# Two transformer blocks in one kernel: deeper attention pipeline, merged output products, and queries and keys scaled after their rotation

## The chip, the cores and the metric

The kernel runs on one core of a Trainium2 chip. The metric is the device time of one execution in microseconds; a lower number is better. Beside it stands a profile of one execution.

## What is computed

A first block of two hybrid layers (causal attention on selected keys, gated linear attention, pooling, a gated feed-forward net) feeds a second block of four mixers of kinds A, B, C, A. The change is mostly about the second. With 512 tokens `x`, 256 context tokens `xc` and 1024 channels, a mixer `i` does this (cut from the reference):

```python
h  = rms_norm_2(x,  norm_g[i]) * (1.0 + sc) + sh          # same for xc with its own sc, sh, gate
u, z = jnp.split(h @ w_in, [n_mix_cols], axis=-1)
q, k = rms_norm_2(q, q_g), rms_norm_2(k, k_g)             # per head of 64; v as it is
q, k = axial_rope(q, ang), axial_rope(k, ang)             # kinds A and C, tokens of x only
p = softmax(q @ k.T * HEAD_DIM ** -0.5)                   # over context and tokens
o = p @ v        # A: 16 heads on 4 key heads;  B: a window of 4 blocks plus a bias, and the context
                 # C: 8 heads, (p0 - lam * p1) @ v, then rms_norm_2 of the result
x = x + gt * ((o * jax.nn.silu(z)) @ w_out)               # xc likewise, except in the last mixer
```

## The kernel before

Every fp32 product is made of three fp16 products: both operands are split into a high and a low half, and hi x hi, hi x lo and lo x hi add up in PSUM (so a weight tile is first split by ScalarE at L372 and VectorE at L373). The program is unrolled; a scheduler then orders the instructions of each engine by a timeline that it simulates, with the order of the code as priority. Generators run side by side: the projections of the next group of heads, the attention of an earlier group (a "channel" that is ticked), and the output product.

A mixer has eight groups of two heads (128 channels). For a group, `pair_job` projects two blocks of 128 columns for two token tiles into one PSUM bank of tag `pj` (two banks). ScalarE evacuates the query or key half into `u` (L1618) and its squares (L1620), VectorE sums the squares (L1621), and GpSimd raises to the power -1/2 (`qny`, L417). Keys are scaled by it (`scale`, L1650), rotated (`rope`: four multiplications by the sine table at L1643, one by the cosine at L1645 on GpSimd, one addition on VectorE at L1646), split in halves by `put_key` (ScalarE cast L1673, GpSimd L1674), and turned by DMA transposes. Queries of kinds A and C are not scaled: their factors are kept as `rq` (L1767) and come in at the softmax. The other halves of the bank become `sz` (L1779, L1780) or the values (L1682, L1683).

`expo` does the first half of an attention item, for one tile of 128 queries and one head: score matmuls into a PSUM tile `S` (two buffers, L680 and L681), the row maximum `mx` (L689), `nm`, which is minus the maximum times the scale (L695; L697 where lambda is added, L704 or L691 elsewhere), and the exponential `P` (L698). `spread` splits `P` in halves `hl` (L715 ScalarE, L716 GpSimd) and turns them into `pt` by one DMA transpose on SyncE's queue (L719), which also issues the weight loads. `slot` keeps the items in a queue: the second half (`pv`, L726 to L728) of an item is issued when more than `skew` items wait. `put_og` makes the operand of the output product, and `out_pair` runs that product, for two groups at a time, with a residual addition per 128 output channels on VectorE (L1577). Pairs 0 and 1 run between the projections of the groups (4 and 6; 3 and 6 in mixer 2), pairs 2 and 3 when the attention has been drained.

In the feed-forward nets of the first block, `ada` computes the second block's modulation; its product and its transposes use the same PSUM bank `T`.

Of the kernel before, what the change touches and what calls it, by code (L numbers as in the profile page):

```python
# [8 lines left out]
F32 = mybir.dt.float32  # L9
# [20 lines left out]
GK = 32.0  # L30

# [14 lines left out]
def constants():  # L46
# [49 lines left out]
def weight_units(a=None):  # L96
# [38 lines left out]
    for i in range(4):  # L135
# [12 lines left out]
        for p in range(4):  # L148
            for n in range(2):
                yield of(("mout", i, p, n), lambda: stack([rows(w, 256 * p + 128 * k, 512 * n, 512) for k in range(2)]))  # L150
# [63 lines left out]
class Kern:  # L214
# [241 lines left out]
    def ada(self):  # L456

        nc, I = self.nc, self.I
        for i in range(4):
            for c in range(6):  # L460
# [10 lines left out]
                pj = self.psT("ad")  # L471
# [19 lines left out]
                self.after(1.0, rest)  # L491
# [140 lines left out]
    def rope_q(self, ps):  # L632
# [4 lines left out]
        nc.scalar.copy(u, ps)  # L637
# [34 lines left out]
    def expo(self, su, q, segs, scale, mask=None, bias=None, add=None):  # L672
# [4 lines left out]
        for off, kh, kl in segs:  # L677
# [3 lines left out]
            nc.tensor.matmul(d, q, kl, start=False, stop=(mask is None))  # L681
            if mask is not None:
                nc.tensor.matmul(d, self.identb, mask, start=False, stop=True)
# [3 lines left out]
        if bias is None:  # L687
            mx = self.sm.tile([128, 1], F32, name="mx")
            nc.vector.reduce_max(mx, s[:, :w], axis=AX.X)  # L689
            if isinstance(scale, float):  # L690
                nc.vector.tensor_scalar_mul(nm, mx, -scale)  # L691
            else:
                scale, neg = scale
                if add is None:
                    nc.vector.tensor_tensor(nm, mx, neg, op=OP.mult)  # L695
                else:
                    nc.vector.tensor_scalar(nm, mx, neg, add, op0=OP.mult, op1=OP.add)  # L697
            nc.scalar.activation(p[:, :w], s[:, :w], AF.Exp, bias=nm, scale=scale, accum_out=su)  # L698
        else:
            mx = self.sm.tile([128, 2], F32, name="mx2")  # L700
            nc.vector.tensor_tensor_reduce(out=p[:, :256], in0=s[:, :256], in1=bias, op0=OP.add, op1=OP.max,
                                           scale=1.0, scalar=-3e38, accum_out=mx[:, 0:1])
            nc.vector.reduce_max(mx[:, 1:2], s[:, 256:512], axis=AX.X)
            nc.vector.tensor_scalar(nm, mx[:, 0:1], mx[:, 1:2], -1.0, op0=OP.max, op1=OP.mult)  # L704
            s2 = self.sm.tile([128, 2], F32, name="su2")
            nc.scalar.activation(p[:, :256], p[:, :256], AF.Exp, bias=nm, accum_out=s2[:, 0:1])
            nc.scalar.activation(p[:, 256:512], s[:, 256:512], AF.Exp, bias=nm, accum_out=s2[:, 1:2])
            nc.vector.tensor_tensor(su, s2[:, 0:1], s2[:, 1:2], op=OP.add)
# [21 lines left out]
    def slot(self, then=None, skew=3):  # L730
# [6 lines left out]
        if len(self.pipe) > skew and self.pipe[0][1]["ok"]:  # L737
            self.pipe.pop(0)[0]()
# [54 lines left out]
    def mixers1(self, l):  # L793
# [4 lines left out]
        self.pipe, self.late = [], []  # L798
        self.kept, self.scored, self.pooled = {0}, False, False
        rt, rb = self.rt, self.rb  # L800
# [135 lines left out]
        def attn(c, qs, kh, kl, vh, vl):  # L936
            for t in range(4):
# [3 lines left out]
                for h in range(2):  # L941
                    w = 128 * (t + 1)
                    pt = self.item(su[:, h:h + 1], qs[:, h, 128 * t:128 * t + 128],
                                   [(0, kh[:, h, :w], kl[:, h, :w])], 0.125, mask=bias[t])
# [40 lines left out]
        for c in range(4):  # L985
# [5 lines left out]
            self.run(unit(C_KA + 128 * c, lambda ps: self.put_k(self.rope_q(ps), kh, kl, S)))  # L991
            self.run(unit(C_QA + 128 * c, lambda ps: self.put_q(self.rope_q(ps), qs, S)))
# [461 lines left out]
    def mixer(self, i):  # L1454
        nc, I = self.nc, self.I
        kind, j, need = i % 3, i // 3, i < 3
        with ExitStack() as es:
# [5 lines left out]
            if kind != 1:  # L1463

                self.rc2 = pl.tile([128, 2, 6, 64], F32, name="rc2", bufs=1)
                self.rs2 = pl.tile([128, 2, 4, 64], F32, name="rs2", bufs=1)
                rot = self.f().rearrange("p (a t d) -> p a t d", a=2, t=4)
                nc.gpsimd.dma_start(rot, I["rot"].rearrange("p (a t d) -> p a t d", a=2, t=4))
                for t, r, g in ((self.rc2[:, :, 0:4], rot[:, 0], 0), (self.rs2, rot[:, 1], 2)):
                    nc.gpsimd.tensor_tensor(t, r.unsqueeze(1).to_broadcast([128, 2, 4, 64]),  # L1470
                                            gv[:, g:g + 2].unsqueeze(2).to_broadcast([128, 2, 4, 64]), op=OP.mult)
                nc.gpsimd.tensor_copy(self.rc2[:, :, 4:6], gv[:, 0:2].unsqueeze(2).to_broadcast([128, 2, 2, 64]))
            else:
# [3 lines left out]
                nc.vector.scalar_tensor_tensor(gv[:, 0], gv[:, 0], 0.125, gv[:, 1], op0=OP.mult, op1=OP.mult)  # L1477
# [4 lines left out]
            self.pipe, self.late = [], []  # L1482
# [23 lines left out]
            for g in range(8):  # L1506
# [10 lines left out]
                if g in ((4,6),(4,6),(3,6),(4,6))[i] and ((4,6),(4,6),(3,6),(4,6))[i][0] == 3:  # L1517
                    self.run(self.out_pair(((4,6),(4,6),(3,6),(4,6))[i].index(g), G, need, i))
            queue.append(None)
            if (1,1,1,1)[i] == 1:  # L1520
                while ca in self.chan:
                    self.tick(1.0)
# [433 lines left out]
```

## Time and profile before

| | |
|---|---|
| median of 3 runs | 2948.93 us (2945.01 to 2952.76) |
| profiled execution | 2949.16 us |
| its span, first to last instruction | 2947.3 us |
| mean granted clock of TensorE, share of full speed | 0.967 |
| busy: TensorE, VectorE, ScalarE, GpSimd | 2633.1, 2126.6, 1665.8, 1530.8 us |

In the rows PE is TensorE's matmul, PEld its weight load, DVE is VectorE, ACT is ScalarE, POOL is GpSimd and SPq is SyncE's queue. `L1577` is a line of the kernel printed above. `out<-in` names tiles. Busy time of an engine is the union of its instructions' spans, and matmuls overlap each other.

### The profile page before, as it was taken

The page shows a single profiled execution, that of the slowest core. Times are in us where ns is not written, and L with a number is a line of the kernel's source. Part 1 is how long each engine was busy: PE and PEld are TensorE (multiplying, and loading weights), DVE is VectorE, ACT ScalarE, POOL GpSimd, SP SyncE. Part 2 cuts the span into 40 slices and gives each one's busy share as a digit, 9 for nine tenths or more (in the row PEclk, how much of TensorE's full clock was granted, in tenths as well). Part 3 has the DMA queues.
Part 4 walks back from the last instruction along what each step waited for, and adds up shares of the span by engine and source line. Part 5 has one row for each costly group of instructions (what it writes and reads, how often), then busy time and mean ns, then how long its engine had stood idle before and what let it go on. Part 6 is the DMA issues. An engine that isn't in the chain of part 4 may idle for free.

```text
span 2947.3 us, 59391 instructions
## 1 busy us (share of the span) xinstructions
PE 2633.1 (89%) x22604; PEld 1760.3 (60%) x22604; DVE 2126.6 (72%) x4155; ACT 1665.8 (57%) x3471; POOL 1530.8 (52%) x1341
## 2 busy tenths in 40 slices
PE   7889999999889999998888799898889898978896
PEld 4554444445554444457666577777677686757564
DVE  5966888437957887346787876767769878786875
ACT  6485555344666655334666656656546555555774
POOL 6763222126754322137766657666656455356774
PEclk9999999999999999999999999999989999989998
DMA  4346565333355564325787637776525546425975
GB/s 155 101 106 153 182 198 185 104 104 103 94 116 179 169 207 155 104 70 120 149 151 149 133 97 151 158 147 135 115 72 107 119 101 122 99 51 129 175 150 113
DMA packets 645167, 385.26 MB, mean 131 GB/s; under 512 B 564510, under 2 KB 574544, under 8 KB 644880
## 3 DMA queue, kind: packets, MB, share of 16 engines
q1 hardware_dynamic: 643328, 378.39, 53.4%
q8 instruction: 177, 2.90, 0.4%
q0 software_dynamic: 1120, 2.88, 0.4%
q14 instruction: 110, 0.90, 0.1%
q10 hardware_dynamic: 432, 0.20, 0.0%
HBM read 232.71 MB, written 2.10 MB: 80 GB/s over the span
## 4 chain that ended last, share of the span: by engine, by line
PE 35%; DVE 24%; DMA 12%; issue 10%; ACT 9%; POOL 9%; SPq 0%; ACTq 0%; DVEq 0%; POOLq 0%
DMA pt<-hl 6%; PE pj L388 5%; PE pj L389 5%; PE pj L390 5%; DVE wlo L373 3%; PE pj L1601 2%; PE pj L1603 2%; PE pj L1602 2%; DVE mx L689 2%; POOL hl L716 2%; ACT P L698 2%; DMA ast<-i_ada_w 2%; POOL qny L417 2%; ACT whi L372 2%; DMA qs<-qst 1%
## 5 line engine op out<-in xcount | busy, mean ns | idle before, releaser
L716 POOL TENSOR_TENSOR hl<-P,hl 128x768 f16<-128x768 f32 (+4 forms) x368 | 474.0, 1294 | 319.8 <-ACT hl L715 257.2
L373 DVE SCALAR_TENSOR_TENSOR wlo<-wst,whi 128x1024 f16<-128x1024 f32 (+1 forms) x292 | 381.4, 1307 | 206.2 <-ACT whi L372 205.3
L1601 PE MATMUL pj<-whi,hh 128*128 128x256 f16 x1664 | 456.0, 274 | 22.8 <-DVE sz L1780 12.5
L1602 PE MATMUL pj<-wlo,hh 128*128 128x256 f16 x1664 | 456.0, 274 | 0.0
L1603 PE MATMUL pj<-whi,hl 128*128 128x256 f16 x1664 | 455.1, 274 | 0.1
L372 ACT ACTIVATE whi<-wst 128x1024 f16<-128x1024 f32 (+1 forms) x292 | 304.3, 1044 | 228.1 <-PE pj L389 130.2
L389 PEld LDWEIGHTS <-whi 128*128 128x128 f16 x1936 | 192.0, 99 | 232.4 <-issue 57.4
L698 ACT ACTIVATE P<-S,nm,rq 128x768 f32<-128x768 f32 (+1 forms) x256 | 225.9, 883 | 171.4 <-DVE nm L695 129.0
L388 PEld LDWEIGHTS <-whi 128*128 128x128 f16 x1936 | 192.2, 99 | 206.4 <-issue 19.9
L390 PEld LDWEIGHTS <-wlo 128*128 128x128 f16 x1936 | 192.2, 99 | 197.1 <-issue 8.0
L689 DVE TENSOR_REDUCE mx<-S 128x1 f32<-128x768 f32 (+4 forms) x352 | 250.2, 718 | 56.2 <-PE S L681 42.5
L715 ACT CAST hl<-P 128x768 f16<-128x768 f32 (+4 forms) x368 | 230.8, 637 | 92.0 <-DMA pt<-hl 58.5
L680 PE MATMUL S<-kh,qs 128*128 128x256 f16 (+3 forms) x672 | 207.0, 315 | 75.6 <-ACT P L698 59.5
L726 PE MATMUL O<-vh,pt 128*128 128x64 f16 (+1 forms) x1472 | 194.0, 202 | 62.0 <-DMA pt<-hl 54.0
L1601 PE MATMUL pj<-whi,mxl 128*128 128x256 f16 x704 | 196.9, 280 | 17.7 <-DVE sz L1780 9.6
L726 PEld LDWEIGHTS <-pt 128*128 128x128 f16 x1536 | 146.5, 101 | 97.8 <-DMA pt<-hl 88.0
L681 PE MATMUL S<-kl,qs 128*128 128x256 f16 (+3 forms) x672 | 197.6, 315 | 0.0
L1602 PE MATMUL pj<-wlo,mxl 128*128 128x256 f16 x704 | 196.8, 280 | 0.9 <-DVE wlo L373 0.9
L1603 PE MATMUL pj<-whi,mxl 128*128 128x256 f16 x704 | 195.5, 280 | 1.6 <-DVE mxl L1444 1.6
L388 PE MATMUL pj<-og,whi 128*128 128x256 f16 (+1 forms) x512 | 163.8, 323 | 37.0 <-DVE mxh L1577 16.1
L727 PE MATMUL O<-vl,pt 128*128 128x64 f16 (+1 forms) x1472 | 193.6, 202 | 0.0
L728 PE MATMUL O<-vh,pt 128*128 128x64 f16 (+1 forms) x1472 | 193.3, 202 | 0.0
(402 smaller groups left out, 7830.0 us busy)
## 6 DMA issues: line engine op xcount, KB each, us to landing
wst<-i_wts SPq DMA_DIRECT2D x318, 512.0 KB
ast<-i_ada_w SPq DMA_DIRECT2D x96, 512.0 KB
wst<-i_wts SPq DMA_DIRECT2D x16, 384.0 KB
pt<-hl SPq DMA_TRANSPOSE x368
rpb<-i_rpb SPq DMA_DIRECT2D x8, 384.0 KB
xin<-i_x SPq DMA_DIRECT2D x4, 512.0 KB
kh<-h SPq DMA_DIRECT2D x32, 64.0 KB
kl<-h SPq DMA_DIRECT2D x32, 64.0 KB
```

Source lines behind the costliest of these rows:

```text
L372: nc.scalar.activation(hi[:, :n], st[:, :n], AF.Copy, scale=s)
L373: nc.vector.scalar_tensor_tensor(lo[:, :n], st[:, :n], s, hi[:, :n], op0=OP.mult, op1=OP.subtract)
L388: nc.tensor.matmul(ps, a, u, start=(k == 0), stop=False)
L389: nc.tensor.matmul(ps, a, v, start=False, stop=False)
L390: nc.tensor.matmul(ps, b, u, start=False, stop=(k == kt - 1))
L689: nc.vector.reduce_max(mx, s[:, :w], axis=AX.X)
L698: nc.scalar.activation(p[:, :w], s[:, :w], AF.Exp, bias=nm, scale=scale, accum_out=su)
L716: nc.gpsimd.tensor_tensor(hl[:, w:2 * w], p[:, :w], hl[:, :w], op=OP.subtract)
L726: nc.tensor.matmul(o, pt[:, i], vh, start=(i == 0), stop=False)
L1601: nc.tensor.matmul(d, hh[:, k, s], hi[:, k % 4], start=(k == 0), stop=False)
L1602: nc.tensor.matmul(d, hh[:, k, s], lo[:, k % 4], start=False, stop=False)
L1603: nc.tensor.matmul(d, hl[:, k, s], hi[:, k % 4], start=False, stop=(k == KD - 1))
```

## The change

It makes these edits. (1) Queue depth `skew`, buffers and the number of `og` tiles grow in the mixers; the SBUF for it comes from a smaller scratch for DMA descriptors. (2) `slot` queues the matmuls of a second half behind the score matmuls of an item `lead` places back. (3) The output product runs in three parts, `OUTS`, of four, two and two groups. (4) Queries carry the softmax scale, so that `expo` has no scale; in kind B they are negated, and a minimum takes the place of the maximum. The first block's queries and keys carry 0.5 and 0.25. (5) The rotation comes before the scaling, with the sine table doubled so that two instructions do what four did. (6) The casts of queries and keys move from ScalarE to VectorE. (7) The mean's factor moves into the squares. (8) `ada`'s product uses bank `O`, and its transposes follow later.

```diff
+OUTS = ((0, 4), (4, 2), (6, 2))
...
-        bm[:, jj] = np.where(ok, 0, -BIG)
+        bm[:, jj] = np.where(ok, 0, BIG)
...
-                pj = self.psT("ad")
+                pj = self.psO("ad")
...
-                self.after(1.0, rest)
+                self.after(4.0, rest)
...
-        nc.scalar.copy(u, ps)
+        nc.scalar.activation(u, ps, AF.Copy, scale=scale)
...
-            nc.tensor.matmul(d, q, kl, start=False, stop=(mask is None))
+            last = nc.tensor.matmul(d, q, kl, start=False, stop=(mask is None))
...
+        self.scores_at.append(last.ins)
...
+            neg = self.negq
+            if neg:
+                nc.vector.tensor_reduce(nm, s[:, :w], axis=AX.X, op=OP.min)
+            else:
+                nc.vector.tensor_reduce(nm, s[:, :w], axis=AX.X, op=OP.max, negate=True)
+            if add is not None:
+                nc.vector.tensor_tensor(nm, nm, add, op=OP.add)
+            nc.scalar.activation(p[:, :w], s[:, :w], AF.Exp, bias=nm, scale=-1.0 if neg else 1.0, accum_out=su)
...
-            nc.vector.reduce_max(mx, s[:, :w], axis=AX.X)
-            if isinstance(scale, float):
-                nc.vector.tensor_scalar_mul(nm, mx, -scale)
...
-                    nc.vector.tensor_tensor(nm, mx, neg, op=OP.mult)
-                else:
-                    nc.vector.tensor_scalar(nm, mx, neg, add, op0=OP.mult, op1=OP.add)
-            nc.scalar.activation(p[:, :w], s[:, :w], AF.Exp, bias=nm, scale=scale, accum_out=su)
...
-            nc.vector.tensor_scalar(nm, mx[:, 0:1], mx[:, 1:2], -1.0, op0=OP.max, op1=OP.mult)
+            nc.vector.tensor_reduce(mx, s[:, 256:512], axis=AX.X, op=OP.min)
+            nc.vector.tensor_tensor_reduce(out=p[:, :256], in0=s[:, :256], in1=bias, op0=OP.add, op1=OP.min,
+                                           scale=1.0, scalar=mx, accum_out=nm)
...
-            self.pipe.pop(0)[0]()
+            fn = self.pipe.pop(0)[0]
+
+            n = len(self.scores_at) - 1 - self.lead * max(len(self.pipe) + 1 - self.gap, 0)
+            with self.tc.issue_after(self.scores_at[n]):
+                fn()
...
+        self.lead, self.gap = 1, 5
...
-                self.rs2 = pl.tile([128, 2, 4, 64], F32, name="rs2", bufs=1)
+                self.rs2 = pl.tile([128, 2, 4, 2, 64], F32, name="rs2", bufs=1)
...
-            self.skew = (5,6,3)[kind]
-            self.pp, self.nbuf, self.wide = pl, ((3,3,6),(3,3,7),(3,2,4))[kind], (NT, S, NT)[kind]
+            self.skew = (7,7,3)[kind]
+            self.pp, self.nbuf, self.wide = pl, ((3,4,8),(3,4,8),(4,3,5))[kind], (NT, S, NT)[kind]
...
+            self.negq = kind == 1
+            self.lead, self.gap = (1, 1, 2)[kind], 5
...
-                if g in ((4,6),(4,6),(3,6),(4,6))[i] and ((4,6),(4,6),(3,6),(4,6))[i][0] > 3:
-                    self.run(self.out_pair(((4,6),(4,6),(3,6),(4,6))[i].index(g), G, need, i))
+                if g == 6:
+                    self.run(self.out_pair(0, G, need, i))
...
+            self.run(self.out_pair(1, G, need, i))
             self.run(self.out_pair(2, G, need, i))
...
-            self.run(self.out_pair(3, G, need, i))
...
-        us = [self.wunit("mout", i, p, n, nk=2, ncol=512, sc=self.wsub) for n in range(2)]
-        og = [[self.og[2 * p + k][n] for k in range(2)] for n in range(2)]
+        m = 1024 // ng
+        us = [self.wunit("mout", i, g0, n, nk=ng, ncol=m, sc=self.wsub) for n in range(1024 // m)]
+        m //= 128
+        og = [[self.og[g0 + k][n] for k in range(ng)] for n in range(2)]
...
-            nc.scalar.activation(sq.rearrange("p (t c) -> p t c", t=2), ps, AF.Square)
+            nc.scalar.activation(sq.rearrange("p (t c) -> p t c", t=2), ps, AF.Square, scale=WI / 8)
...
-        for h in range(2):
-            for b in range(2):
-                k = slice(2 * h, 2 * h + 2)
-                self.nc.gpsimd.tensor_tensor(o[:, :, k, b], a[:, :, k, 1 - b], r[:, :, :, b], op=OP.mult)
+        for b in range(2):
+            self.nc.gpsimd.tensor_tensor(o[:, :, :, b], a[:, :, :, 1 - b], r[:, :, :, b], op=OP.mult)
...
-        nc.scalar.copy(s[:, :, :, 0], v)
+        nc.vector.tensor_copy(s[:, :, :, 0], v)
...
-        nc.scalar.copy(a, v)
+        nc.vector.tensor_copy(a, v)
...
-            self.scale(u, 6, y)
             if kind != 1:
                 self.rope(u, 6, 1)
+            self.scale(u, 6, y)
...
-            rq = st["rq"] = pl.tile([128, 2, 6, 2], F32, name="rq")
-
             def then(u, y):
-                for k in range(2):
-                    nc.vector.tensor_scalar_mul(rq[:, k, :n4], y, 0.125 - 0.25 * k)
+                nc.vector.tensor_scalar_mul(y, y, 0.125)
                 self.rope(u, n4, 0)
+                self.scale(u, n4, y)
                 self.put_query(u, n4, qs)
...
-        og = pl.tile([128, 2, NT], F16, name="og", bufs=4)
+        og = pl.tile([128, 2, NT], F16, name="og", bufs=6)
...
-    nc = _bacc.Bacc("TRN2", target_bir_lowering=False, num_devices=1)
+    nc = _bacc.Bacc("TRN2", target_bir_lowering=False, num_devices=1, dynamic_dma_scratch_size=1024)
```

## Rows read from the trace of the kernel before

**Rows 1.** Windows, one per mixer: span, busy PE, PEld, DVE, ACT, POOL; PEclk, DMA.

```profile
1303.00:1692.00 389.00, 326.32 (x3483) 253.25 (x3481) 287.90 (x578) 232.07 (x503) 262.32 (x247) 0.96 0.66 131
1692.00:2140.00 448.00, 400.77 (x4066) 332.05 (x4066) 318.11 (x855) 263.06 (x743) 285.38 (x288) 0.98 0.64 134
2140.00:2627.00 487.00, 430.29 (x3765) 345.40 (x3764) 390.43 (x857) 277.72 (x693) 243.43 (x209) 0.96 0.46 100
2627.00:2947.30 320.30, 259.44 (x2779) 199.66 (x2777) 232.26 (x419) 187.04 (x367) 208.59 (x188) 0.94 0.66 134
```

**Rows 2.** Timeline of PE inside mixer 0: start, duration, instruction; eight starts apart.

```profile
1562.35 0.27 PE L1601 MATMUL pj<-whi,mxl 128*128 128x256 f16 x1
...
1563.22 0.27 PE L1603 MATMUL pj<-whi,mxl 128*128 128x256 f16 x1
```

**Rows 3.** Waits of PE in the second block: us in total, times, longest us.

```profile
PE S L680 <- ACT P L698: 52.8, 55, 3.2
PE O L726 <- DMA pt<-hl: 44.6, 57, 2.5
PE pj L1601 <- DVE sz L1780: 22.0, 6, 10.6
PE pj L1601 <- DVE vl L1683: 16.9, 9, 7.5
PE pj L388 <- DVE mxh L1577: 16.1, 17, 2.7
PE pj L388 <- DVE x L1577: 14.2, 10, 3.7
```

**Rows 4.** Waits of ACT in the second block.

```profile
ACT P L698 <- DVE nm L695: 129.0, 82, 6.4
...
ACT qst L1659 <- DVE u L1646: 39.3, 16, 5.7
ACT kst L1673 <- DVE u L1646: 32.2, 8, 11.8
...
ACT P L698 <- DVE nm L697: 27.6, 23, 5.9
ACT P L706 <- DVE nm L704: 27.5, 22, 4.8
```

**Rows 5.** Timeline at the start of mixer 3; in brackets the idle time before.

```profile
2683.10 0.83 ACT L1673 CAST kst<-u 128x768 f16<-128x768 f32 x1 [5.86 <-issue]
...
2685.33 0.39 PE L1601 MATMUL pj<-whi,hh 128*128 128x256 f16 x1 [10.56 <-DVE sz L1780]
```

**Rows 6.** Groups by line and shape: busy us, mean ns; idle before and releasers.

```profile
L695 DVE TENSOR_TENSOR nm<-mx,rq 128x1 f32<-128x1 f32 x208 | 97.2, 469 | 1.5
...
L1643 POOL TENSOR_TENSOR f<-u,rs 128x128 f32<-128x128 f32 x144 | 77.3, 566 | 22.4 <-ACT u L1618 11.1 <-DVE u L1650 7.4 <-DVE qss L1627 3.7
...
L1577 DVE SCALAR_TENSOR_TENSOR x<-pj,aG,x 128x512 f32<-128x512 f32 x96 | 71.3, 744 | 15.4 <-PE pj L390 15.1
...
L1577 DVE SCALAR_TENSOR_TENSOR mxh<-pj,aG,mxh 128x256 f32<-128x256 f32 x96 | 44.6, 475 | 7.8 <-PE pj L390 7.6
...
L1650 DVE TENSOR_TENSOR u<-u,qny 128x768 f32<-128x768 f32 x28 | 37.5, 1341 | 21.7 <-POOL qny L417 21.7
...
L1767 DVE TENSOR_SCALAR rq<-qny 128x12 f32<-128x12 f32 x32 | 20.8, 687 | 11.0 <-POOL qny L417 11.0
...
L704 DVE TENSOR_SCALAR nm<-mx 128x1 f32<-128x1 f32 x64 | 12.8, 204 | 0.3
L697 DVE TENSOR_SCALAR nm<-mx,rq,lams 128x1 f32<-128x1 f32 x48 | 12.7, 265 | 0.3
```

**Rows 7.** Single lines: durations in ns, least, median, most; first and last start.

```profile
L695 DVE TENSOR_TENSOR nm<-mx,rq x208: 138/160/1777, 1370.2 to 2911.9; 128x1 f32<-128x1 f32 x104
...
L607 DVE CAST f<-f x1: 420/420/420, 11.5 to 11.5; 128x512 f32<-128x512 int32 x1
```

**Rows 8.** Waits of PE over the whole span.

```profile
PE T L482 <- ACT adev L477: 9.1, 10, 1.8
```

More of the change, by code (lines that the diff above doesn't have):

```diff
@@ L147, in weight_units @@
         w = A["abc"[kind] + "_w_out_2"][j] if a else None
-        for p in range(4):
-            for n in range(2):
-                yield of(("mout", i, p, n), lambda: stack([rows(w, 256 * p + 128 * k, 512 * n, 512) for k in range(2)]))
+        for g0, ng in OUTS:
+            for n in range(4 if ng == 4 else 2):
+                m = 1024 // ng
+                yield of(("mout", i, g0, n), lambda: stack([rows(w, 128 * (g0 + k), m * n, m) for k in range(ng)]))
 def layout(inp):
@@ L630, in rope1, with rope_q @@
             nc.vector.tensor_copy(self.g1[:, 8 * n:8 * n + 8], self.vec1[:, at:at + 8])
-    def rope_q(self, ps):
+    def rope_q(self, ps, scale=1.0):
         nc = self.nc
@@ L670, in item, with expo @@
         return self.spread(*self.expo(*a, **k))
-    def expo(self, su, q, segs, scale, mask=None, bias=None, add=None):
+    def expo(self, su, q, segs, mask=None, bias=None, add=None):
         nc = self.nc
@@ L680, in expo @@
             nc.tensor.matmul(d, q, kh, start=True, stop=False)
-            nc.tensor.matmul(d, q, kl, start=False, stop=(mask is None))
+            last = nc.tensor.matmul(d, q, kl, start=False, stop=(mask is None))
             if mask is not None:
-                nc.tensor.matmul(d, self.identb, mask, start=False, stop=True)
+                last = nc.tensor.matmul(d, self.identb, mask, start=False, stop=True)
+        self.scores_at.append(last.ins)
         w = segs[-1][0] + segs[-1][1].shape[-1]
@@ L990, in mixers1 @@
             vl = pm.tile([128, 4, 128], F16, name="vl", bufs=2)
-            self.run(unit(C_KA + 128 * c, lambda ps: self.put_k(self.rope_q(ps), kh, kl, S)))
-            self.run(unit(C_QA + 128 * c, lambda ps: self.put_q(self.rope_q(ps), qs, S)))
+            self.run(unit(C_KA + 128 * c, lambda ps: self.put_k(self.rope_q(ps, 0.25), kh, kl, S)))
+            self.run(unit(C_QA + 128 * c, lambda ps: self.put_q(self.rope_q(ps, 0.5), qs, S)))
             self.run(tunit(C_VA + 128 * c, lambda ps: put_v(ps, vh, vl)))
@@ L1570, in out_pair @@
             d = slice(t0, t0 + nt)
-            if p == 3 and need:
+            if final and need:
                 acc = self.tmp.tile([128, NC_], F32, name="acc", tag="acc", bufs=2)
@@ L1574, in out_pair @@
                 ps = self.psA()
-                yield from self.mm_fm(ps[:, :nt], [us[o // 4]], 128 * (o % 4), og[0], og[1], at, at + nt, (1, 0))
+                yield from self.mm_fm(ps[:, :nt], [us[o // m]], 128 * (o % m), og[0], og[1], at, at + nt, tuple(reversed(range(ng))))
                 yield self.left
                 nc.vector.scalar_tensor_tensor(x[:, o, d], ps[:, :nt], G[:, k, o:o + 1], x[:, o, d], op0=OP.mult, op1=OP.add)
-                if p == 3 and need:
+                if final and need:
                     self.square(acc, o, x[:, o, d])
-            if p == 3 and need:
+            if final and need:
                 self.norm_h(acc, v, n)
-            elif p == 3:
+            elif final:
                 self.store(n)
@@ L1879, in attn_group @@
                 q = qs[:, h, 128 * t:128 * t + 128]
-                scale = 1.0 if kind == 1 else [st["rq"][:, k, t, h:h + 1] for k in range(2)]
                 if kind != 2:
-                    pt = self.item(su[:, h:h + 1], q, segs, scale, bias=bias)
+                    pt = self.item(su[:, h:h + 1], q, segs, bias=bias)
                     def second(t=t, h=h, pt=pt, su=su, vb=vb):
@@ L1900, in attn_group @@
                 else:
-                    p, w = self.expo(su[:, h:h + 1], q, segs, scale, add=None if h else self.lams[:, 1:2])
+                    p, w = self.expo(su[:, h:h + 1], q, segs, add=None if h else self.lams[:, 1:2])
                     cs.append(p)
```

58 lines of the change are left out of this document (26 added, 32 removed).

## The prediction

> **What bounds the kernel now.** I read the stages first, by windows [rows 1]. The second block is the four mixers, 1303 to 2947.3 us. Their TensorE is busy 326.3, 400.8, 430.3 and 259.4 us, so it idles 62.7, 47.2, 56.7 and 60.9 us, 227.5 us together. All other engines are less busy than TensorE in each mixer, but VectorE stands at 74, 71, 80 and 73%, GpSimd at 67, 64, 50 and 65%: nothing has a floor above TensorE, and all are coupled by in-order queues. The granted clock is 0.96, 0.98, 0.96 and 0.94 there; the shares below full speed are worth 0.04 x 389 + 0.02 x 448 + 0.04 x 487 + 0.06 x 320.3 = 63 us.
>
> The second view is the timeline of TensorE in a dense place: matmuls with 256 columns start every 0.109 us (eight of them in 0.87 us), though each record lasts 0.27 us [rows 2]. So where TensorE is fed it runs at pitch, and only feeding it better can help; gaps below some 0.16 us don't even count as idle. The Trainium skill (Perfetto Trace Analysis, section Identifying the Most-Contended Engine) says that busy time of matmuls is a poor measure of the distance to the roofline. By that rule more than 227.5 us is open; these records agree.
>
> Third come TensorE's waits in the second block [rows 3]: 52.8 us at a score matmul for the exponential that frees its PSUM bank, 44.6 us at P x V for the DMA transpose of the probabilities, 38.9 us (22.0 + 16.9) at a projection for the evacuation of its bank, 30.3 us (16.1 + 14.2) at an output matmul for the residual add that frees its bank. Fourth, what makes the exponential late: ScalarE waited 129.0 + 27.6 + 27.5 = 184.1 us for `nm`, the little VectorE operation behind the row maximum [rows 4]. It also stood 39.3 and 32.2 us in front of the casts of queries and keys, whose input VectorE had not added yet [rows 4]. What such a cast does stands in a timeline [rows 5]: ScalarE reaches the key cast after 5.86 us, evacuations stand behind it in the queue, and TensorE loses 10.56 us at the start of mixer 3.
>
> **The change part by part.** *Scores.* Queries now carry the scale, so maximum and negation are one reduction. Gone are 208 operations of 0.469 us (97.2 us), 64 of 0.204 (12.8) and 48 of 0.265 (12.7) [rows 6]; where mixer 2 needs its lambda, 48 adds of the first kind come, 48 x 0.469 = 22.5 us (22.5 at the mean, 7.7 at the median of 0.160 [rows 7]). Net 100 us of VectorE, and all of it lay between score and exponential. The first block loses the like; I leave that at nothing (0 to 64 x 0.204 = 13 us of VectorE that is no bound there).
>
> *Scaling.* The two `rq` operations per group become one: 24 x 0.65 = 16 us less [rows 6]. 24 query groups get a full scaling instead: 16 x 1.341 + 8 x 0.894 (two thirds of it, 512 columns for 768) = 28.6 us more [rows 6]. For keys it only moves behind the rotation, so the rotation need not wait for the norm. The rotation on GpSimd takes two instructions where it took four: 144 x 0.566 = 82 us [rows 6] become 72 of between 0.566 and 1.132 us; at 0.85 that is 20 us less (0 to 41). No instruction reads PSUM that did not before: the input is still the copy in SBUF.
>
> *Casts.* 44 of 768 columns and 8 of 512 go from ScalarE to VectorE. The nearest row is VectorE's one-input cast of 512 columns, 0.420 us, 0.63 for 768 in proportion; above, the two-input operation of 768 columns at 1.341 [rows 6, 7]. The tiny `nm` shows what waiting adds here: 0.160 median, 0.469 mean, 1.777 at most [rows 7], so I add 0.31: 44 x 0.94 + 8 x 0.73 = 47 us (31 to 66). ScalarE is rid of casts and of standing before them.
>
> *Merged outputs.* Four groups accumulate in one bank, then twice two. Matmuls and weight bytes stay. Per mixer 8 adds of 0.744 us go, and 8 of 0.475 in three mixers: 32 x 0.744 + 24 x 0.475 = 35 us of VectorE [rows 6]. What moves is the time: the first output now runs at group 6, its first half no longer at group 4 (3 in mixer 2), so attention of the groups between has only projections to fill TensorE. I cost that at nothing, because the same matmuls still fill the place at group 6; bare of them it is part of the slow case below.
>
> VectorE in sum: 97.2 + 12.8 + 12.7 + 16 + 35 = 174 less, 22.5 + 28.6 + 47 = 98 more, net 76 us less (56 to 107). In mixer 2 it is about even, since its `nm` waits little and it takes 16 casts and 8 scalings.
>
> *Depth.* P x V of an item follows seven items after its score, before five (mixers 0 and 3) or six (mixer 1); mixer 2 keeps three, with one more buffer for each of three tiles. P x V is now pinned behind a score: the third before the newest where the queue is deep, the newest in mixer 2 and the first block. *Side edits.* The modulation's product takes another bank and its transposes come later; TensorE waits 9.1 us there [rows 8]. The smaller DMA scratch has no row; few transfers use the GpSimd queue, at starts of stages. I take 0, at most one start stall of 10.6 us [rows 3].
>
> Now TensorE's time. (a) Waits at scores: 100 of the 184 us that ScalarE waited for `nm` go, 54%; 52.8 x 0.54 = 29 us (0 to 53). (b) Waits for transposes: 44.6 us in 57, 0.78 us each. One more item of 768 keys puts at least 6 x 0.109 = 0.65 us of scores between [rows 2], two put 1.3; at the same depth nothing. I take 60%, 27 us (0 to 45). (c) Projection waits: the key chain before the bank is shorter and ScalarE no longer blocks, but VectorE still does; a third, 13 us (0 to 39). (d) 56 of 256 residual adds go, so 22% of 30.3, 7 us. (e) 7 of the 9.1 us. Sum 83. Of this 76 lies in the second block, a third of its idle time; a third of the clock's 63 us comes back, 21. That makes 104 us.
>
> I don't forecast all of it, because a wait that goes uncovers the next. The measure for what stays is mixer 1, which has no such `nm`: it idles 47.2 us for 400.8 busy, 0.118. If the others fall to that ratio, mixer 0 gains 62.7 - 38.5 = 24, mixer 2 57 - 51 = 6, mixer 3 60.9 - 30.6 = 30: 60 us. I take 60 of the 104. Profiled execution 2949.16 us (span 2947.3 and 1.9 around it; 0.2 above the median of the runs) less 60 gives **2889 us**, with a range of its own of 2855 to 2925.
>
> **Rivals.** *All of it arrives* (0.12): the deep queue absorbs what is uncovered too; 2949 - 104 = 2845, 2820 to 2855. For it: no engine is full in a whole mixer. Against: in-order queues.
>
> *The port eats it* (0.14). VectorE's moved work waits on GpSimd and makes GpSimd wait. For it: `nm`, one column wide, took 0.138 us at best and 1.777 at worst, and its mean is three times its median [rows 6, 7]. The new casts and scalings are such operations, mixer 2 gets no relief, and (a) and (c) fail. There remain b, d and e, 41 us, of which by the same 60 of 104 some 24 arrive: 2925, with 2925 to 2945. Beside it: the Trainium skill (SBUF — State Buffer, section SBUF: two separate sides) calls the port pair that VectorE and GpSimd share an exclusive lock, which a VectorE operation in two-port mode or with two SBUF inputs takes whole. The spread of `nm` agrees; whether a cast takes it, no row of before shows.
>
> *Slower: the pin* (0.14). TensorE is in order. A score that waits for its bank now holds the P x V pinned behind it, whose data are there; before, it could run first. Place: the 55 waits at scores [rows 3]. Price: 18 matmuls of 64 columns, a quarter of 0.109 each, 0.49 us; 55 x 0.49 = 27 us more, and if waits at scores stay, a and c don't come and the deeper queue is blocked, with d and e at 8 us: 2949 + 27 - 8 = 2968. It decides once more than some 40 waits at scores remain and the held products are ready. Against: in three mixers the pin is three items back, which binds only a product that ran early.
>
> **How the numbers follow.** Forecast 0.60. Within 0.3% (about 9 us, what a measurement of this kernel can tell from no change) is 2940 to 2958. The forecast and the full gain are faster; of the port case 0.09 is faster and 0.05 the same; the pin is slower except 0.01. So 0.81 faster, 0.06 same, 0.13 slower. The range from 2825 to 2955 leaves out the pin and the far end of the full gain, under 0.2.
>
> **What would show it.** `nm` as an operation is gone and ScalarE's wait for the reduction is below 110 us; TensorE's wait at scores falls below 30, at transposes below 20. VectorE's busy time in the mixers falls by some 75 us. The casts on VectorE take 0.6 to 1.0 us; if they take over 1.3, or GpSimd's split grows, the port case is on. TensorE idle in mixers 0 and 3 falls to about 38 and 31 us, in mixers 1 and 2 little. The pin would show as waits at scores of the old size with P x V directly behind them. What would make me wrong: a new wait on VectorE for GpSimd's rotation in front of the evacuations, or a worse order around group 6.

## The result and the profile after

The changed kernel takes 2919.21 us (median of 4 runs, 2916.71 to 2920.66) beside 2950.85 us for the kernel before (4 runs): a ratio of 0.9894, 95% interval [0.9875, 0.9912], 31.6 us faster. The forecast was 2889, so the sign was right, the time lies inside the forecast's own range of 2855 to 2925, and about half of the 60 us came. The profiled execution took 2916.71 us with a span of 2914.8.

First the windows of the changed kernel, one per mixer (columns as in [rows 1]; each is cut where the last output product of a mixer ends, so the first starts at 1283.4, and the last holds the tail):

```profile
1283.40:1681.50 398.10, 335.08 (x3591) 264.31 (x3588) 262.74 (x495) 223.09 (x509) 264.62 (x231) 0.94 0.66 133
1681.50:2117.10 435.60, 391.84 (x4055) 328.29 (x4052) 318.05 (x750) 241.28 (x716) 290.03 (x285) 0.99 0.66 135
2117.10:2612.80 495.70, 431.78 (x3768) 348.24 (x3767) 397.39 (x818) 258.57 (x684) 243.90 (x182) 0.95 0.44 97
2612.80:2914.80 302.00, 253.59 (x2781) 196.41 (x2779) 208.71 (x352) 174.61 (x351) 205.52 (x165) 0.96 0.71 143
```

The difference of second and first number is TensorE's idle time: 63.0, 43.8, 63.9 and 48.4 us, 219 together; [rows 1] gave 227.5. Only mixer 3 clearly gained (60.9 to 48.4); mixer 0, forecast at 38, still idles 63, and mixer 2 idles more than before.

Idle time is the smaller part of the gain. When the kernel before is cut in the same way, its mixers run from 1293.4 to 2947.3 us, and the sums over the four mixers are, before and then after:

```profile
sum 1653.90, PE 1426.41 PEld 1138.99 DVE 1234.69 ACT 964.17 POOL 1001.61; mean PE 356.60 PEld 284.75 DVE 308.67 ACT 241.04 POOL 250.40
```

```profile
sum 1631.40, PE 1412.28 PEld 1137.25 DVE 1186.88 ACT 897.55 POOL 1004.07; mean PE 353.07 PEld 284.31 DVE 296.72 ACT 224.39 POOL 251.02
```

The span is 32.5 us shorter in these two profiles. Of that, 22.5 us lie in the mixers: 8.4 us are idle time of TensorE, and 14.1 us are its busy time, at the same number of matmuls (a record lasts longer than the pitch [rows 2], so busy time covers short gaps). The other 10.0 us lie in the first block, which the prediction left at nothing; single profiles do not tell them from chance (see E8). VectorE's busy time in the mixers fell by 47.8 us, where 76 were forecast.

Next TensorE's waits in the second block, the answer to [rows 3]:

```profile
PE S L685 <- ACT P L701: 43.7, 47, 3.4
PE O L728 <- DMA pt<-hl: 29.4, 29, 3.6
PE pj L1610 <- DVE sz L1786: 25.5, 7, 11.6
PE pj L1610 <- DVE vl L1691: 20.7, 13, 5.8
```

Scores fell by 9 us (52.8 to 43.7) and transposes by 15 (44.6 to 29.4), but projections wait for VectorE's evacuations 46.2 us, where it was 38.9. And ScalarE's waits there, the answer to [rows 4]:

```profile
ACT P L701 <- DVE nm L698: 85.0, 58, 8.4
...
ACT P L701 <- DVE nm L700: 66.5, 42, 4.6
...
ACT P L708 <- DVE nm L705: 50.4, 27, 4.4
...
ACT P L701 <- DVE nm L696: 38.9, 11, 9.8
ACT u L1627 <- POOL klt L1682: 37.9, 4, 16.7
```

The operation behind the maximum is gone, yet ScalarE does not wait less for the maximum: its four rows sum to 240.8 us, and before they summed to 210.8, the 184.1 of the prediction and one row that [rows 4] leave out:

```profile
ACT P L698 <- DVE nm L691: 26.7, 17, 4.3
```

The last row is new in size: in four places an evacuation of a projection stands for the tile `u`, which GpSimd's split of the keys still holds. The longest is at the start of mixer 0:

```profile
1339.73 0.38 ACT L1627 ACTIVATE u<-pj 128x256 f32<-128x256 f32 x1 [16.72 <-POOL klt L1682]
```

Little of it is the cast, which takes 0.55 us at 1336.8; until 1334.7 GpSimd is busy without a break with roots, tables and the rotation.

Last the groups by line and shape, the answer to [rows 6]:

```profile
L700 DVE TENSOR_TENSOR nm<-nm,lams 128x1 f32<-128x1 f32 x48 | 20.1, 419 | 0.0
...
L1651 POOL TENSOR_TENSOR f<-u,rs 128x256 f32<-128x256 f32 x72 | 57.8, 823 | 34.9 <-ACT u L1627 24.4 <-issue 10.4
...
L1586 DVE SCALAR_TENSOR_TENSOR x<-pj,aG,x 128x512 f32<-128x512 f32 x64 | 47.8, 748 | 39.1 <-PE pj L394 38.9
...
L1586 DVE SCALAR_TENSOR_TENSOR mxh<-pj,aG,mxh 128x256 f32<-128x256 f32 x72 | 33.6, 475 | 11.0 <-PE pj L394 10.6
...
L1658 DVE TENSOR_TENSOR u<-u,qny 128x768 f32<-128x768 f32 x44 | 59.8, 1360 | 14.7 <-POOL qny L1638 14.2
...
L1658 DVE TENSOR_TENSOR u<-u,qny 128x512 f32<-128x512 f32 x8 | 10.4, 1296 | 0.1
...
L1667 DVE CAST qst<-u 128x768 f16<-128x768 f32 x24 | 17.3, 719 | 1.1 <-DMA kh<-kst 0.9
L1667 DVE CAST qst<-u 128x512 f16<-128x512 f32 x8 | 7.0, 875 | 0.1
L1681 DVE CAST kst<-u 128x768 f16<-128x768 f32 x20 | 13.6, 680 | 0.1
```

The parts have the forecast's sizes: the lambda's adds 20.1 us (forecast 22.5), the rotation 77.3 to 57.8, 19.5 less (20), the residual adds 34.5 less (35), the scalings 32.7 more (28.6), the casts 17.3 + 7.0 + 13.6 = 37.9 us (47). VectorE's balance has not, since the record of a small operation lies in part over that of another, and busy time counts such a moment once; and what the parts do to TensorE's time was not.

### The profile page after: what moved, and what is told of

It is laid out like the page before. It is cut to its first block, busy times and chain, and to the rows that moved or that the text cites. A ratio compares the mean times of both kernels' runs of the same rounds, so it can differ in the third digit from the quotient of the medians.

```text
span 2914.8 us, 58866 instructions
## 1 busy us (share of the span) xinstructions
PE 2620.5 (90%) x22604; PEld 1761.4 (60%) x22604; DVE 2067.9 (71%) x3783; ACT 1598.5 (55%) x3419; POOL 1533.4 (53%) x1272
## 5 line engine op out<-in xcount | busy, mean ns | idle before, releaser
L1610 PE MATMUL pj<-whi,hh 128*128 128x256 f16 x1664 | 455.8, 274 | 26.6 <-DVE sz L1786 13.6
L701 ACT ACTIVATE P<-S,nm 128x768 f32<-128x768 f32 (+4 forms) x352 | 251.2, 716 | 221.0 <-DVE nm L698 106.3
L394 PEld LDWEIGHTS <-wlo 128*128 128x128 f16 x1936 | 191.7, 99 | 198.6 <-issue 10.7
L698 DVE TENSOR_REDUCE nm<-S 128x1 f32<-128x768 f32 (+4 forms) x320 | 235.9, 749 | 47.0 <-PE S L686 35.6
L1610 PEld LDWEIGHTS <-hh 128*128 128x128 f16 x1664 | 163.9, 98 | 35.9 <-DVE sz L1786 13.2
```

The costliest lines, as they stand in the source:

```text
L698: nc.vector.tensor_reduce(nm, s[:, :w], axis=AX.X, op=OP.max, negate=True)
L1610: nc.tensor.matmul(d, hh[:, k, s], hi[:, k % 4], start=(k == 0), stop=False)
```

## Experiments

Times are medians of four runs each. The kernels ran on several chips, so differences between them are taken from their ratios to the kernel before, times 2950; with their intervals combined, such a difference is good to 7 us, where either kernel is one of E5 to E8 to 10 or 11.

Each edit also makes the scheduler order the whole program anew. Of ScalarE's some 2310 instructions from 1275 us on, about 16% stand in another order in E5 than in E1, 8% in E10 and 2% in E11 (those outside the longest common order of the two traces). So a difference is the price of an edit together with the order that came with it, and no run here separates the two.

| kernel | us | ratio, 95% interval | difference |
|---|---|---|---|
| changed | 2919.21 | 0.9894 [0.9875, 0.9912] | |
| E1 casts on ScalarE | 2890.21 | 0.9790 [0.9774, 0.9806] | -31 to changed |
| E2 output in four pairs | 2922.28 | 0.9903 [0.9888, 0.9918] | +3 to changed |
| E3 no pin | 2920.48 | 0.9899 [0.9884, 0.9914] | +1 to changed |
| E4 shallow | 2913.15 | 0.9874 [0.9859, 0.9889] | -6 to changed |
| E5 = E1 + operation after the maximum | 2915.58 | 0.9893 [0.9863, 0.9924] | +30 to E1 |
| E6 = E1 + shallow | 2909.50 | 0.9868 [0.9840, 0.9895] | +23 to E1 |
| E7 = E6 + idle casts on VectorE | 2921.85 | 0.9907 [0.9884, 0.9930] | +12 to E6 |
| E8 = E1 + scaling on GpSimd in mixer 2 | 2886.68 | 0.9785 [0.9756, 0.9814] | -1 to E1 |
| E9 = E8 + shallow buffers in mixer 2 | 2891.59 | 0.9792 [0.9777, 0.9807] | +1 to E1 |
| E10 = E1 + idle casts on VectorE | 2913.20 | 0.9870 [0.9855, 0.9884] | +24 to E1 |
| E11 = E1 + modulation as before | 2906.28 | 0.9844 [0.9830, 0.9859] | +16 to E1 |
| E12 = E1 + scaling before rotation | 2901.67 | 0.9826 [0.9809, 0.9842] | +11 to E1 |

### E1: the casts back on ScalarE

```diff
-        nc.vector.tensor_copy(s[:, :, :, 0], v)
+        nc.scalar.copy(s[:, :, :, 0], v)
...
-        nc.vector.tensor_copy(a, v)
+        nc.scalar.copy(a, v)
```

> The changed kernel with the casts of queries and keys back on ScalarE, all else as changed. My theory (the casts stood in front of evacuations on ScalarE, term c, 13 us): 2925 to 2935 us, and ScalarE's waits for VectorE's addition in front of the casts are back at some 70 us. Rival (the port: the casts on VectorE cost more than they free): 2900 to 2912 us, VectorE busy 30 us less. If neither: within 5 us of 2919.

Measured: 31 us faster than the changed kernel, in the rival's direction and beyond its range. Its waits in the second block, first of TensorE, then of ScalarE:

```profile
PE S L685 <- ACT P L701: 37.0, 42, 2.2
PE pj L1610 <- DVE sz L1786: 24.2, 8, 10.2
PE O L728 <- DMA pt<-hl: 22.9, 22, 3.4
...
PE pj L1610 <- DVE vl L1691: 15.3, 10, 5.4
```

```profile
ACT P L701 <- DVE nm L698: 58.6, 43, 7.9
...
ACT kst L1681 <- DVE u L1658: 36.4, 15, 12.4
...
ACT qst L1667 <- DVE u L1658: 31.9, 20, 3.1
...
ACT u L1627 <- POOL klt L1682: 12.3, 4, 4.6
```

Every wait that the forecast wanted smaller is smaller than in the changed kernel: scores 37.0 for 43.7, transposes 22.9 for 29.4, evacuations 39.5 for 46.2 (38.9 before the change, so these gained nothing). ScalarE's four waits for a maximum sum to 181.1 us (58.6 + 56.3 + 34.9 + 31.3). It again stands 36.4 + 31.9 us in front of the casts, much as in the kernel before, and it costs less than freeing it of them did. The wait for the buffer `u` falls from 37.9 to 12.3, but at the start of mixer 0 it only has another name:

```profile
1342.70 0.83 ACT L1681 CAST kst<-u 128x768 f16<-128x768 f32 x1 [12.37 <-DVE u L1658]
```

Behind this cast the evacuation of `u` starts 15.4 us after ScalarE's instruction before the wait had ended; in the changed kernel it was 16.7. There ScalarE waits for the chain of the keys in both, with the casts or without.

### E2, E3, E4: the merged outputs, the pin, the depth

```diff
-OUTS = ((0, 4), (4, 2), (6, 2))
+OUTS = ((0, 2), (2, 2), (4, 2), (6, 2))          # E2, run at groups 4, 6 and behind the last
...
-            with self.tc.issue_after(self.scores_at[n]):
-                fn()
+            fn()                                 # E3
...
-            self.skew = (7,7,3)[kind]
+            self.skew = (5,6,3)[kind]            # E4, and E6
...((3,4,8),(3,4,8),(4,3,5))[kind] -> ((3,3,6),(3,3,7),(3,2,4))[kind]
```

> The changed kernel with the output product in four parts of two groups again, at groups 4 and 6 and two at the end. My theory (term d, fewer residual additions): 7 us slower, about 2926 us, VectorE 35 us busier. Rival (the merged product took work for TensorE away from the groups in the middle and eats the gain of mixers 0 and 2): 10 to 25 us faster, 2895 to 2910, most of it in mixers 0 and 2.

> The changed kernel without the edge that queues second halves behind scores. If the pin costs (my slow case): up to 27 us faster, 2892 to 2910, with less waiting at scores. If the pin does nothing here: within 5 us of 2919. If it is what made transposes come in time: 10 us slower or more, with TensorE's wait for transposes back above 40 us in the second block.

> The changed kernel with the queue depth and the buffers of before (5, 6, 3). My theory (term b, 27 us of which some 60% arrive): 2930 to 2940 us, TensorE's wait for transposes in the second block back from 29 to about 45 us. Rival (depth buys nothing, the gain is the shorter score path): within 5 us of 2919.

Measured: +3, +1 and -6 us. Merged outputs and pin can't be told from nothing. The depth, forecast as 27 us of transposes, bought nothing in the changed kernel. TensorE's wait for transposes in E3 shows that their fall is not the depth's alone:

```profile
PE O L728 <- DMA pt<-hl: 49.7, 42, 2.9
```

Without the pin they wait 49.7 us for 29.4 with it, at the same depth, while evacuations wait 32.7 for 46.2, and the time is the same. E3's expectation had tied a wait above 40 us to a loss of 10 us or more; the wait came and the loss did not.

### E6: the depth, with the casts on ScalarE

The edit is E4's on top of E1's.

> The changed kernel with the casts on ScalarE (2890.21 us), and the depth of the pipeline and the numbers of buffers of the kernel before in the first two kinds of mixer and in the third. Theory of the prediction, term (b): the depth is worth some 15 to 27 us, so 2905 to 2917 us. Theory after the run with the shallow pipeline alone (2913.15 against 2919.21): the depth gives nothing or costs a little, 2880 to 2893 us, most likely 2885, with the fourth mixer some 9 us longer and the third some 6 us shorter than with the deep one. I hold the second for likelier, 80 to 20.

Measured: 23 us slower than E1. I had held the other outcome for likelier; it missed. Depth is worth nothing with the casts on VectorE and 23 us with them on ScalarE. TensorE's waits for transposes in the second block say where: in the shallow kernels, E4 and then E6,

```profile
PE O L728 <- DMA pt<-hl: 38.6, 45, 2.6
```

```profile
PE O L728 <- DMA pt<-hl: 39.8, 43, 2.6
```

they are equal. Depth takes them to 29.4 in the changed kernel and to 22.9 in E1, 9 and 17 us less. The waits for evacuations rise with it in both, by 10.8 us in the changed kernel (20.4 + 15.0 in E4, 46.2 with depth) and by 8.3 in E1 (18.3 + 12.9 in E6, 39.5 with depth). So the two waits together cancel in the changed kernel and fall by 9 us in E1. That has the sign of the 23 us and not their size.

### E5: an operation after the maximum

```diff
             if add is not None:
                 nc.vector.tensor_tensor(nm, nm, add, op=OP.add)
+            else:
+                nc.vector.tensor_scalar_mul(nm, nm, 1.0)
...
+            nc.vector.tensor_scalar_mul(nm, nm, 1.0)     # behind the one with a bias
```

> The changed kernel with the casts on ScalarE (2890.21 us), plus one VectorE operation on a column of 128 values after every row maximum that has no added term: the multiplication by one stands between the maximum and the exponential, where the kernel before had its scaling of the maximum. Nothing else is undone. Theory of the prediction, term (a): each of these operations stood on the chain from the scores to the exponential and its removal is worth 17 to 29 us of the whole; this kernel then takes 2907 to 2919 us, and the wait of the matmuls of the scores on the exponential grows from 37 us to 60 or more. Rival: the chain is covered by the items in flight, the operation costs only VectorE some 45 us of its spare time, and the time stays at 2886 to 2895 us. I hold the first for likelier, 65 to 35.

Measured: 30 us slower than E1. The groups of the new operation (line 702 without, 709 with the bias), and ScalarE's wait for it in the second block:

```profile
L702 DVE TENSOR_SCALAR nm<-nm 128x1 f32<-128x1 f32 x304 | 42.5, 144 | 1.6
...
L709 DVE TENSOR_SCALAR nm<-nm 128x1 f32<-128x1 f32 x64 | 8.9, 145 | 0.4
```

```profile
ACT P L703 <- DVE nm L702: 109.4, 76, 7.4
...
ACT P L703 <- DVE nm L700: 37.8, 25, 4.5
...
ACT P L711 <- DVE nm L709: 27.8, 20, 3.4
```

51.4 us of VectorE's records, in operations of 0.144 us each, cost 30 us of the span, the price of term (a). By VectorE's time it is not explained: most of these records lie over those of other operations, and VectorE's busy time in the mixers rises by 4.8 us (1172.7 to 1177.6). In E5's profile mixers 0 and 3 are 9.0 and 10.7 us longer than in E1's, the others by about 1. The waits don't show the path either. The 109.4 us stand against 58.6 + 31.3 = 89.9 in E1, since line 702 stands behind both of those maxima, and ScalarE's waits for a maximum in all are 175.0 us for 181.1. TensorE's wait at scores goes from 37.0 to 44.7, where 60 or more was expected. So the price agrees with term (a), and the path by which it is paid is not shown.

### E7 and E10: casts that nobody waits for

```diff
         nc.scalar.copy(s[:, :, :, 0], v)
+        nc.vector.tensor_copy(idle[:, :n4], v)           # the same behind the cast of the keys
```

The tile `idle` is a buffer of its own in E7, and a work tile of the ring in E10.

> The shallow kernel with the casts on ScalarE, plus a copy on VectorE of the same size, type and place as each cast of queries and of keys, into a buffer that nothing reads. The chain from the projection to the transposes thus keeps its casts on ScalarE, and VectorE does all the work that it does in the changed kernel, in the same order. Theory one, the queue of VectorE: the cast costs because the maxima of the scores stand behind it (and its port is contended), whoever waits for its result; the time is then within 6 us of the shallow kernel with casts on VectorE, 2907 to 2919 us. Theory two, the chain: the cast costs because it ends late on a busy VectorE, so that the transposes and the group's scores start late; an idle copy then costs almost nothing, at most 8 us over the shallow kernel with casts on ScalarE, about 2885 to 2893 us. 55 to 45.

> The deep changed kernel with the casts on ScalarE (2890.21 us), plus a copy on VectorE of the size, type and place of each cast, into a work tile that nothing reads. In the shallow kernels such a copy cost 12 us. Theory one, the queue of VectorE: what the casts on VectorE cost in the deep kernel (29 us) is the time that the row maxima stand behind them, so 2910 to 2925 us here, and the waits of the scores' matmuls on the exponentials go back from 37 to 44 us or more in the second block. Theory two, the chain: the casts' own results come late, the idle copies cost 12 us at most as in the shallow kernels, 2890 to 2903 us. 50 to 50.

Measured: E7 is 12 us slower than E6 (good to 11, and some 3 us above the range of theory one), E10 24 us slower than E1. So in the deep kernel the same work on VectorE, with the results on ScalarE as before, can cost 24 us, where the casts on VectorE cost 31. The copies and TensorE's wait at scores in E10:

```profile
L1668 DVE CAST f<-u 128x768 f16<-128x768 f32 x24 | 17.9, 747 | 0.2
...
L1683 DVE CAST f<-u 128x768 f16<-128x768 f32 x20 | 14.4, 722 | 0.2
...
L1668 DVE CAST f<-u 128x512 f16<-128x512 f32 x8 | 6.7, 839 | 0.2
```

```profile
PE S L685 <- ACT P L701: 49.4, 44, 5.0
```

39.0 us of copies, 0.2 us idle before each group: VectorE comes to them from other work, and the maxima are late; the wait at scores goes from 37.0 to 49.4, and ScalarE's four waits for a maximum from 181.1 to 201.3 (68.5 + 64.6 + 34.2 + 34.0). That the 24 us are part of the same 31 is not shown. Over E1's profile, E10's is longer by 0.4, 7.0, 8.0 and 7.3 us in the four mixers, the changed kernel's by 15.4, 9.4, 2.5 and 3.4. In the shallow kernels the idle casts cost more (12) than the casts themselves (2, E4 against E6); that ScalarE is also rid of its own there may be the reason, and no run shows it.

### E8 and E9: the third mixer

```diff
+                self.scale(u, n4, y, nc.gpsimd if kind == 2 else nc.vector)   # queries, E8 and E9
...((3,4,8),(3,4,8),(4,3,5))[kind] -> ((3,4,8),(3,4,8),(3,2,4))[kind]        # E9
```

> The changed kernel with the casts on ScalarE (2890.21 us), with the scaling of the queries in the third mixer alone on GpSimd instead of VectorE: 8 operations of 768 columns, 1.3 us each on VectorE. Theory one: the third mixer is longer than in the kernel before because VectorE, busy four fifths of it, has taken on these scalings; without them the third mixer falls from 493.1 to 484 us or less, and the whole to about 2881 us. Rival: they are not on the path, or the operation is longer on GpSimd (some 2 us by its products of the same width) and lengthens the chain of the queries by as much as it saves: the third mixer stays within 4 us of 493 us, the whole within 4 us of 2890 us. 35 to 65.

> The changed kernel with the casts on ScalarE, the scaling of the third mixer's queries on GpSimd (2886.68 us so far), and for the third mixer alone the numbers of buffers of the kernel before; the deep pipeline stays in the others. In two pairs of kernels that differ in all depths the third mixer was 6.0 us shorter with the shallow numbers (489.8 against 495.8, 487.2 against 493.1). Theory: the fewer, differently shared buffers of that mixer save it 6 us here too, third mixer 478 us, the whole 2878 to 2884 us. Rival: what both pairs show is the way the second mixer hands over to the third, and the third mixer stays within 3 us of 484 us, the whole within 4 us of 2887 us. 60 to 40.

Measured: no difference to E1 in either. The window of mixer 2 is shorter in E8's profile,

```profile
2097.40:2581.50 484.10, 426.32 (x3769) 346.27 (x3767) 374.11 (x790) 268.52 (x696) 255.40 (x188) 0.97 0.46 100
```

484.1 us for 493.2 in E1, with VectorE 21 us less busy, but the whole did not follow. E9's rests on the same: 481.8 us there and nothing in the total. Among the profiles of the eleven kernels whose first block is the same code, its end lies anywhere from 1283.0 to 1293.5 us, so one profile does not tell 9 us of a stage from chance.

### E11: the modulation's bank

```diff
-                pj = self.psO("ad")
+                pj = self.psT("ad")
...
-                self.after(4.0, rest)
+                self.after(1.0, rest)
```

> The changed kernel with the casts on ScalarE (2890.21 us), with the products of the modulation in the bank that they had in the kernel before and their second half one unit of work later, as there, and not four. Theory of the prediction, term (e): the other bank is worth 7 us, so 2895 to 2899 us, all of it in the first block's stretches (1289.1 us with the new bank, by that 1294 to 1299). Rival: the modulation's products are hidden either way, within 4 us of 2890 us, and what the first block gained (293.4 to 283.4 us past 1000) is from the operation that its row maxima lost. 35 to 65.

Measured: 16 us slower than E1, twice the forecast's term (e), which I had held for the less likely outcome. But not for the reason given. TensorE's waits there over the whole span, in E1 and then in E11:

```profile
PE T L486 <- ACT adev L481: 8.4, 11, 2.0
```

```profile
PE T L486 <- ACT adev L481: 7.4, 9, 1.8
...
PE ad L478 <- DVE adt L489: 2.4, 1, 2.4
...
PE ad L478 <- DVE ms L534: 1.5, 1, 1.5
...
PE ad L478 <- ACT mxh L1310: 0.8, 1, 0.8
```

The wait of [rows 8], 9.1 us before, is still there in E1 (8.4). What went are waits for the bank, 4.7 us. E11's profiled execution is its fastest, 10.7 us slower than E1's, and of that only 2.3 us lie ahead of the mixers. The rest is spread over the four mixers (2.5, 2.7, 0.5 and 2.5 us), whose code is the same in both; why is not settled.

### E12: scaling first

```diff
+            self.scale(u, 6, y)
             if kind != 1:
                 self.rope(u, 6, 1)
-            self.scale(u, 6, y)                          # the queries likewise
```

> The changed kernel with the casts on ScalarE (2890.21 us), with each tile of queries and of keys scaled before it is rotated (second mixer: before its weights), as the keys were in the kernel before; the same operations in another order. Theory of the prediction, term (c): rotating first takes the reciprocal root off the chain of the keys and queries, and is worth up to 6 us, so 2893 to 2900 us. Rival one: the root is computed on GpSimd ahead of the rotation, in the same queue, so the order changes nothing, within 4 us of 2890 us. Rival two: scaling first lets VectorE scale while GpSimd is not yet on that tile and takes the scaling off the end of the chain, 2880 to 2886 us. 25, 55, 20.

Measured: 11 us slower than E1, beyond what any of the three wanted, nearest to the first. TensorE's waits in the second block:

```profile
PE O L728 <- DMA pt<-hl: 34.9, 38, 2.4
...
PE pj L1610 <- DVE vl L1691: 23.7, 13, 3.8
```

Transposes wait 34.9 us for 22.9 in E1, evacuations of values 23.7 for 15.3; the scores do not wait longer (33.1). E12's profiled execution is the slowest of its four (2909.55 us, the median is 2901.67), so these rows overstate the difference. Rotating first is worth having; by which chain, they do not decide.

## Why the prediction was half right

**The failed step is the casts, in term (c).** The prediction said that "the key chain before the bank is shorter and ScalarE no longer blocks, but VectorE still does", and took 13 us of gain. TensorE's waits there did not fall: 38.9 us before, 46.2 in the changed kernel, 39.5 in E1; and at the start of mixer 0 the evacuation on ScalarE came after 16.7 us without the casts in its queue and after 15.4 with them. The prediction had the casts' duration (47 us forecast, 37.9 measured) only in VectorE's balance, where the removed operations outweighed it, and gave it no price in time. E1 prices the move: 31 us lost, about what the forecast was missed by (60 against 31.6). E10 shows that such work on VectorE can cost 24 us even when nobody waits for its result, with the maxima later. How the 31 us divide between the place in VectorE's queue, the lateness of the casts' own results and the new order of the program stays open.

**The rest of the sum was near.** With the casts left on ScalarE the change makes 0.9790, 62 us, where 60 was forecast for all of it. That the two meet is in part luck, since the terms came by other ways than forecast.
- (a) Forecast 29 us; E5 gives 30. The signs named for it failed: TensorE's wait at scores, forecast below 30, is 37.0 in E1, and ScalarE's wait for the reduction, forecast below 110, is 181.1 in E1 and 240.8 in the changed kernel. Without the operation, ScalarE waits for the maximum itself.
- (b) Forecast 27; E6 gives 23 with the casts on ScalarE, E4 nothing with them on VectorE. Transposes, forecast below 20, wait 22.9 us in E1 and 29.4 in the changed kernel; there the waits for evacuations rose by as much as depth saved.
- (c) Other than the casts, E12 gives the order 11 us.
- (d) Forecast 7; E2 gives 3, not told from nothing, though 34.5 us of VectorE went.
- (e) Forecast 7; E11 gives 16, with the wait that was named still there.
- The clock: 21 of 63 us were forecast to come back. By the same sum over the windows the shares below full speed are worth 65 us in the changed kernel and 57 in E1 (granted 0.97, 0.98, 0.95 and 0.96 there), so nothing came there, and some 7 us in E1.

These parts sum to 30 + 23 + 11 + 3 + 16 = 83 us, more than the 62 that E1 gains. So each, taken out alone, costs more than its share. That fits the prediction's argument for its step from 104 to 60, that a wait that goes uncovers the next; a new order with each edit would fit as well. The measure used there, mixer 1's idle ratio, was not borne out: mixer 0 stayed at 63.0 us and 55.0 even in E1, not 38. It was no measure of what stays, either: mixer 1 did have such operations, 64 at L704 and 32 at L691, and without them it idles 34.0 us in E1, not 47.2.

**The rivals.** *The port eats it* came nearest in time (2925), and half of it holds, that VectorE's moved work eats gain; the port has a small part in it. Its own signs did not appear: the casts took 0.68 to 0.88 us on average, not over 1.3, and GpSimd's splits of keys and queries stayed at 1.76 and 1.64 us for 768 columns (1.73 and 1.65 before). Least, median and most of the casts of queries are

```profile
L1667 DVE CAST qst<-u x32: 412/560/1747, 1357.8 to 2856.5; 128x768 f16<-128x768 f32 x24, 128x512 f16<-128x512 f32 x8
```

The Trainium skill (SBUF — State Buffer, section SBUF: two separate sides) makes the shared port an exclusive lock; the 1.747 us at most agrees with a cast that stood before it, the median of 0.560 says that most did not. The longest cast and the GpSimd operation beside it:

```profile
2855.90 2.09 POOL L718 TENSOR_TENSOR hl<-P,hl 128x768 f16<-128x768 f32 x1
2856.53 1.75 DVE L1667 CAST qst<-u 128x512 f16<-128x512 f32 x1
```

The cast ends 0.28 us after that operation. Each of the 16 casts of keys and queries that took more than 0.65 us ran beside such a two-input operation of GpSimd and ended 0.28 us (512 columns) or 0.41 to 0.42 us (768) after it; together they lost 10.0 of the 37.9 us against casts left alone (0.41 and 0.55 us). And (a), which that rival gave up, came by its price in E5. *The pin* is excluded by E3: +1 us. *All of it arrives* did not, not even in E1.

**Open** stays why mixer 2 is longer in the changed kernel (495.7 for 487 us). Its scalings, its buffers and the order of rotation each moved it by 2 to 9 us in single profiles, and E8 and E9 moved the whole by nothing. Open is also where E11's 16 us lie, and how the 24 us of E10 divide between the place in the queue, the port and the new order.

**A faster version** than the changed kernel is E1, with E8 and E9 equal to it within their intervals: 2890.21 us, 2.1% under the kernel before.

## What to carry to other kernels

Price an operation by what stands behind it in the queue it enters, not by the engine's busy share or busy time: VectorE was busy only 66 to 80% in the mixers, yet 39.0 us of copies that nobody read cost 24 us of the whole (E10), and one-column operations between maximum and exponential cost 30 us though they made VectorE only 4.8 us busier there (E5), while 34.5 us of residual adds elsewhere were worth 3, not told from nothing. An engine that stands waiting in front of an operation, as ScalarE did for the casts, is no reason to move the operation; ask what stands behind it in the other queue. And test parts together as well as alone: the depth was worth 23 us or nothing, by where the casts ran. In a program whose order a scheduler makes, a change of some us can be the new order; in E11 most of 10.7 us lay in stages whose code had not changed.

## Not expected of the hardware

In these traces an exponential whose scale is a column of a tile is longer than one with a constant scale. The groups before, then after:

```profile
L698 ACT ACTIVATE P<-S,nm,rq 128x768 f32<-128x768 f32 x192 | 190.0, 990 | 122.7 <-DVE nm L695 101.2 <-DVE nm L697 8.6 <-DVE ri L1889 7.4
```

```profile
L701 ACT ACTIVATE P<-S,nm 128x768 f32<-128x768 f32 x192 | 172.7, 901 | 117.9 <-DVE nm L698 68.4 <-DVE nm L700 45.1 <-DVE qny L1772 1.7
```

0.990 against 0.901 us for 768 columns, 192 times: 17 us of ScalarE that the prediction did not count.
